# Block 0's heads transposed in pairs from one tile, masks of later blocks on GpSimd, no GpSimd power at the close

## The chip, the cores and the metric

The kernel runs on one core of a Trainium2 chip. A core has five engines with queues of their own, each worked off in order: TensorE (matrix products into PSUM), VectorE and ScalarE (elementwise work), GpSimd (elementwise work in SBUF, and DMA issue) and SyncE (DMA issue). The metric is the device time of one execution in microseconds; lower is better.

## The reference, cut to what matters

One decoder layer on 2048 tokens of width 1024, in float32. A joint projection feeds 8 stick-breaking attention heads (dimension 64) and 4 heads of gated linear attention; both outputs are normalised per head, joined, projected and added to the input; a ConvFFN follows and a last norm.

```python
def reference(x, ...):
    h = rms_norm(x, attn_norm_g[l])
    proj = h @ w_in[l]
    sb_q, sb_k, sb_v, g_q, g_k, g_v, g_lr, g_og = jnp.split(proj, offsets, axis=-1)
    o_sb = head_rms_norm(stick_breaking_attention(sb_q, sb_k, sb_v), sb_out_g[l])
    o_gla = head_rms_norm(gla_chunked(g_q, g_k, g_v, log_a), gla_out_g[l]) * jax.nn.silu(g_og)
    x = x + jnp.concatenate([o_sb, o_gla], axis=-1) @ w_out[l]
    h = rms_norm(x, ffn_norm_g[l])
    u = causal_depthwise_conv(h @ w_ffn_up[l], conv_w[l], conv_b[l])
    a, val = jnp.split(u, 2, axis=-1)
    x = x + (jax.nn.silu(a) * val) @ w_ffn_down[l]
    return rms_norm(x, final_norm_g)

def stick_breaking_attention(...):   # per block of queries; strict is s < t
    log1m = jnp.where(strict, -jax.nn.softplus(z), 0.0)
    after = lax.cumsum(log1m, axis=3, reverse=True) - log1m
    w = jnp.where(strict, jnp.exp(jax.nn.log_sigmoid(z) + after), 0.0)
    o = w @ v
```

## The kernel before, in words

Tokens are cut in 4 blocks of 512 (`NB`, `TB`), each in 4 row tiles of 128. Every float32 product is made of three passes over a high and a low half (`split_psum`, `split_w`: ScalarE rounds the high half, VectorE or GpSimd subtracts for the low one).

The stages follow each other: (1) norm of the input and transposes (`prep`, lines 189 to 208), where the norm's vector `gat` comes by GpSimd's DMA queue (line 195); (2) projections to DRAM, with the gated linear attention woven in (`gla`); (3) the output gate (`og_group`) of the 16 row tiles, with the attention of block 0 woven in from block 1 of the gate on; (4) for each block the output product, the FFN and the norm (`ffn`), with the attention of blocks 1 to 3 woven in by a running clock (lines 912 to 931).

Attention goes by steps (`attention_steps`). A step makes the weights of one row tile against one key block of 512: scores on TensorE, on the diagonal a matmul that adds a mask of -1e30 (line 529), two sigmoids on ScalarE (`m` and `wt`, lines 531 and 533), a product scan over `m` on VectorE (line 537) and `wt` times the scan (line 543). Five steps later (`LAG`) the weights are transposed (line 554), then multiplied with the values (lines 569 and 570). When a head is complete, `finish` transposes it back (line 580), squares it on GpSimd (585), takes mean and power there (86 and 88), scales it on VectorE (591), and SyncE stores it to the DRAM tile `osc` (593). Key and value tiles come by GpSimd's queue into a ring of buffers (line 517), as does the query (514).

`o_feat` makes the left operand of the output product: SyncE loads 128 of the 1024 features of a block from `osc` (line 620), TensorE transposes (623), and the halves are split (96 and 97). In block 0, `FEAT` says at which attention step and row tile each feature is made; feature 3 (heads 6 and 7) is made inside the output product (`LATE`, line 794).

`accumulate` is the output and the down product: two column halves `n`, eight (or seven) chunks `ci` of weights, each loaded, split and, in block 0, stored split for the later blocks (lines 720 to 731). Behind the last chunk VectorE adds the residual (765), ScalarE squares (768), VectorE sums (774), GpSimd raises to the power -0.5 (775), and `result` scales and stores.

TensorE's order is the program's. The queues of the other engines are ordered by a planner from simulated times, so an edit can re-order them elsewhere too.

Of the kernel before, what the change touches and what calls it, by code (L numbers as in the profile page):

```python
# [8 lines left out]
F32 = mybir.dt.float32  # L9
# [7 lines left out]
P = 128  # L17
# [25 lines left out]
FEAT = {4: (10, (2, 0)), 5: (12, (2, 0)), 6: (14, (2, 0)), 7: (16, (2, 0)),  # L43
        0: (26, (3, 0)), 1: (31, (3, 0)), 2: (38, (3, 0))}
# [5 lines left out]
def hybrid_block_kernel(ctx, tc, x, attn_norm_g, w_in, w_gate_up, b_gate_up, sb_out_g,  # L50
# [66 lines left out]
    if True:  # L117
# [11 lines left out]
        def n_tile(shape, name):  # L129
            return low.tile(shape, F32, tag="n", name=name, bufs=3)  # L130
# [55 lines left out]
        with tc.tile_pool(name="xp", bufs=2, side="right") as xp, tc.tile_pool(name="sm", bufs=2, side="right") as sm:  # L186
            gat = m1_tile([P, D], F32, "gat")

            def prep(b):
                for t in range(4):  # L190
# [3 lines left out]
                    if r0 == 0:  # L194
                        nc.gpsimd.dma_start(out=gat, in_=attn_norm_g.to_broadcast([P, D]))
# [108 lines left out]
        ams = [n_tile([P, 2, P], f"am{i}") for i in range(2)]  # L304
        for zt in [*qbd, *ams, *(sts[j][0] for j in range(NPAIR))]:
            nc.vector.memset(zt.bitcast(F32), 0.0)
# [165 lines left out]
    ohring = Ring([n_tile([P, 4, HD], f"oh{i}") for i in range(2)])  # L472
# [7 lines left out]
    def early_memory(q1):  # L480

        a0 = slot(0, [P, 4, TB], F32, "wtA")
        a1 = slot(1, [P, 4, TB], F32, "wtB")
        a2 = slot(2, [P, 2, 2, TB], F32R, "kvA")
        a3 = slot(3, [P, 2, 2, TB], F32R, "qA")
        tri = []
        for n, (whole, shared) in enumerate(((a0[:, 0, :], a0[:, 1, :]), (a0[:, 3, :], a1[:, 0, :]))):
            tri += [shared[:, 384:512], a0[:, 2, n * 256:(n + 1) * 256], shared[:, 0:384], whole]
        pring = Ring([a1[:, 2, :], a1[:, 3, :]])
        return ((Ring(tri), pring, Ring([a2[:, 0], a2[:, 1], a3[:, 1]]), Ring([q1, a3[:, 0]]), a1[:, 1, :]),  # L490
                (a0, a1, a2, a3, pring))
# [7 lines left out]
    def attention_steps(blocks, rings, behind=1, banks=None):  # L499
# [8 lines left out]
        def make_weights(u, t):  # L508
# [16 lines left out]
            for l in range(2):  # L525
                nc.tensor.matmul(z[:, :width], qt[:, l, t * P:(t + 1) * P], kt[:, 0, :width],  # L526
                                 start=(l == 0), stop=(l == 1 and not diag))
            if diag:
# [4 lines left out]
            nc.scalar.activation(wt[:, :width], z[:, :width], AF.Sigmoid, scale=0.125)  # L533
            pp = pring.next()[:, lo:TB]
# [41 lines left out]
        def finish(u, asb):  # L576
# [16 lines left out]
            nc.sync.dma_start(out=osc[i][:, h * HD:(h + 1) * HD].rearrange("(t p) d -> p t d", p=P), in_=oh)  # L593
# [20 lines left out]
    q1 = c1.enter_context(tc.tile_pool(name="q1", bufs=1, side="right")).tile([P, 2, TB], F32R, name="q1")  # L614
    early, shared = early_memory(q1)

    def o_feat(b, f, psum, tag, ot=None):
        if ot is None:
            ot = otring.next()
        nc.sync.dma_start(out=ot, in_=osc[b][:, f * P:(f + 1) * P].rearrange("(t p) d -> p t d", p=P))  # L620
# [16 lines left out]
    for b in range(NB):  # L637
        for t in range(4):
            for part, _ in enumerate(og_group(b, t)):
                if b > 0:  # L640

                    while steps < (16 * (b - 1) + 4 * t + part + 1) * FIRST // 46:
# [65 lines left out]
    def accumulate(lhs, w_rows, kept, b, squares=None, extra=None, stagger=False, rstds=None, rows=None, first=None):  # L708
# [5 lines left out]
        for n in range(2):  # L714
# [5 lines left out]
            def load(ci):  # L720
# [38 lines left out]
            for t in range(4):  # L759
# [6 lines left out]
                if squares is not None:  # L766
# [5 lines left out]
                    else:  # L772
                        r = rstds[0][:, t:t + 1]
                        nc.vector.tensor_tensor(out=r, in0=squares[:, t, 1:2], in1=squares[:, t, 0:1], op=ALU.add)
                        nc.gpsimd.tensor_tensor(out=r, in0=r, in1=nhalf[:, 0:1], op=ALU.pow)
                if R:
                    yield 0.65 * R

    def ffn(b, oT, rows, nextT):
# [51 lines left out]
        for gi, G in enumerate(GROUPS):  # L831
# [49 lines left out]
            yield from accumulate(gts, w_ffn_down[ch0 * P:(ch0 + G) * P, :], [w[ch0:ch0 + G] for w in wdn], b, squares=sq2 if final else None,  # L881
                                  extra=extra, stagger=final and last, rstds=[r2])
# [76 lines left out]
```

## Time and profile before

| | us |
|---|---|
| three timed runs | 2795.53, 2797.81, 2800.07 |
| median | 2797.81 |
| profiled execution | 2793.75 |
| its span, first to last instruction | 2791.8 |
| TensorE busy in the span | 2709.1 |

The profile shows one execution. The page gives the busy time of each engine and the costliest groups of instructions; the other views are lists of waits, windows of time, the chain of waits that ended last, and timelines. Matmuls are pipelined, so that a matmul's length is longer than its distance to the next one: the distance counts.

### The profile page before, as it was taken

The page shows a single profiled execution, that of the slowest core. Times are in us where ns is not written, and L with a number is a line of the kernel's source. Part 1 is how long each engine was busy: PE and PEld are TensorE (multiplying, and loading weights), DVE is VectorE, ACT ScalarE, POOL GpSimd, SP SyncE. Part 2 cuts the span into 40 slices and gives each one's busy share as a digit, 9 for nine tenths or more (in the row PEclk, how much of TensorE's full clock was granted, in tenths as well). Part 3 has the DMA queues.
Part 4 walks back from the last instruction along what each step waited for, and adds up shares of the span by engine and source line. Part 5 has one row for each costly group of instructions (what it writes and reads, how often), then busy time and mean ns, then how long its engine had stood idle before and what let it go on. Part 6 is the DMA issues. An engine that isn't in the chain of part 4 may idle for free.

```text
span 2791.8 us, 35920 instructions
## 1 busy us (share of the span) xinstructions
PE 2709.1 (97%) x13096; PEld 2249.1 (81%) x13096; DVE 1678.1 (60%) x2758; ACT 1144.5 (41%) x2364; POOL 542.7 (19%) x754
## 2 busy tenths in 40 slices
PE   8999999999799999999999999999999999999998
PEld 6878888878578778887888888888888888888886
DVE  5246755457487586777776777767767334342333
ACT  5455533235365355554443444445434222221112
POOL 2001212114455455433110000110100000000000
PEclk9999999999899999999999999999999999999999
DMA  6215635467567777768455455574454656555552
GB/s 187 94 62 175 232 136 160 115 184 247 210 210 249 248 238 245 244 232 286 153 185 187 165 181 168 184 250 157 170 175 161 221 191 222 206 196 194 193 192 75
DMA packets 260896, 529.00 MB, mean 189 GB/s; under 512 B 59152, under 2 KB 149360, under 8 KB 238192
## 3 DMA queue, kind: packets, MB, share of 16 engines
q1 hardware_dynamic: 229472, 389.86, 42.9%
q0 software_dynamic: 31248, 136.85, 13.7%
q8 instruction: 103, 1.69, 0.2%
q14 instruction: 73, 0.60, 0.1%
HBM read 384.04 MB, written 142.61 MB: 189 GB/s over the span
## 4 chain that ended last, share of the span: by engine, by line
PE 86%; DVE 5%; DMA 4%; POOL 2%; issue 1%; ACT 1%; SPq 0%; POOLq 0%; ACTq 0%; DVEq 0%
PE ups L848 11%; PE ups L849 11%; PE ups L850 11%; PE d L738 7%; PE d L739 7%; PE d L740 7%; PE z L526 4%; PE tp L554 4%; PE mm L166 3%; PE mm L164 3%; PE mm L165 3%; PE acc L570 2%; PE mm L176 2%; PE mm L175 2%; PE mm L174 2%; PE acc L569 2%
## 5 line engine op out<-in xcount | busy, mean ns | idle before, releaser
L848 PE MATMUL ups<-h2h,u 128*128 128x512 f32 x1408 | 554.3, 394 | 5.0 <-DVE x L765 5.0
L849 PE MATMUL ups<-h2l,u 128*128 128x512 f32 x1408 | 550.7, 391 | 0.0
L850 PE MATMUL ups<-h2h,u 128*128 128x512 f32 x1408 | 549.4, 390 | 0.0
L94 DVE TENSOR_TENSOR ws<-tp,ws 128x512 fp32r<-128x512 f32 (+1 forms) x320 | 194.1, 607 | 202.7 <-ACT ws L93 201.8
L848 PEld LDWEIGHTS ups<-h2h,u 128*128 128x128 f32 x1408 | 265.0, 188 | 61.6 <-DVE x L765 5.6
L850 PEld LDWEIGHTS ups<-h2h,u 128*128 128x128 f32 x1408 | 264.8, 188 | 57.5
L849 PEld LDWEIGHTS ups<-h2l,u 128*128 128x128 f32 x1408 | 265.0, 188 | 54.6
L738 PE MATMUL d<-d,g 128*128 128x512 f32 x736 | 292.0, 397 | 2.5 <-ACT d L101 1.2
L93 ACT ACTIVATE ws<-tp 128x512 fp32r<-128x512 f32 (+1 forms) x320 | 170.0, 531 | 293.9 <-PE tp L554 290.0
L739 PE MATMUL d<-d,g 128*128 128x512 f32 x736 | 288.9, 392 | 0.9 <-POOL d L102 0.9
L740 PE MATMUL d<-d,g 128*128 128x512 f32 x736 | 288.3, 392 | 0.0
L860 DVE SCALAR_TENSOR_TENSOR ct<-ups,cwb,ct 128x511 f32<-128x511 f32 x176 | 131.8, 749 | 251.1 <-POOL ct L859 197.3
L855 ACT ACTIVATE ct<-ups,cwb 128x512 f32<-128x512 f32 x176 | 136.3, 775 | 340.6 <-PE ups L850 340.4
L537 DVE TENSOR_TENSOR_SCAN wtB<-mt,cy 128x512 f32<-128x512 f32 x192 | 250.3, 1304 | 3.0 <-ACT mt L531 2.8
L765 DVE TENSOR_TENSOR x<-d,x 128x512 f32<-128x512 f32 x128 | 85.8, 685 | 165.5 <-PE d L740 165.4
L531 ACT ACTIVATE mt<-z 128x512 f32<-128x512 f32 (+2 forms) x320 | 170.5, 533 | 13.3 <-DVE cy L541 8.0
L859 POOL TENSOR_TENSOR ct<-ct,hadd 128x2 f32<-128x2 f32 x132 | 26.6, 202 | 744.5 <-ACT halo L857 332.4
L738 PEld LDWEIGHTS d<-d,g 128*128 128x128 f32 x736 | 138.4, 188 | 33.4 <-ACT d L101 1.6
L740 PEld LDWEIGHTS d<-d,g 128*128 128x128 f32 x736 | 138.4, 188 | 31.1
L739 PEld LDWEIGHTS d<-d,g 128*128 128x128 f32 x736 | 138.5, 188 | 30.5 <-POOL d L102 1.5
L164 PE MATMUL mm<-hh,w 128*128 128x512 f32 x384 | 151.3, 394 | 0.0
L165 PE MATMUL mm<-hl,w 128*128 128x512 f32 x384 | 150.2, 391 | 0.0
(242 smaller groups left out, 5341.9 us busy)
## 6 DMA issues: line engine op xcount, KB each, us to landing
u<-wup SPq DMA_DIRECT2D x132, 1024.0 KB, 4.7
d<-wdn SPq DMA_DIRECT2D x94, 512.0 KB, 3.4
wup<-u POOLq DMA_DIRECT2D x44, 1024.0 KB, 6.7
kvA<-kvs POOLq DMA_DIRECT2D x54, 512.0 KB, 4.8
uraw<-in_w_ffn_up_dram SPq DMA_DIRECT2D x44, 512.0 KB, 4.8
wdn<-d POOLq DMA_DIRECT2D x44, 512.0 KB, 4.9
d<-wou SPq DMA_DIRECT2D x38, 512.0 KB, 4.2
dw<-wdn SPq DMA_DIRECT2D x38, 512.0 KB, 3.8
```

Of the source, the lines that this page charges most:

```text
L93: nc.scalar.activation(hi, ps, AF.Copy)
L94: nc.vector.tensor_tensor(out=lo, in0=ps, in1=hi.bitcast(F32), op=ALU.subtract)
L164: nc.tensor.matmul(ps, whi[k][:, fs], hh[b][k // 4][:, k % 4, :], start=(k == 0), stop=False)
L165: nc.tensor.matmul(ps, whi[k][:, fs], hl[b][k // 4][:, k % 4, :], start=False, stop=False)
L531: nc.scalar.activation(m[:, lo:TB], z[:, :width], AF.Sigmoid, scale=-0.125)
L537: nc.vector.tensor_tensor_scan(out=pp[:, ::-1], data0=mr, data1=mr, initial=1.0 if prev is None else prev, op0=ALU.mult, op1=ALU.bypass)
L738: nc.tensor.matmul(accs[t], gh[:, ts], whi, start=(ci == 0), stop=False)
L739: nc.tensor.matmul(accs[t], gh[:, ts], wlo, start=False, stop=False)
L740: nc.tensor.matmul(accs[t], gw[:, ts], whi, start=False, stop=(ci == G - 1))
L848: nc.tensor.matmul(ps, whi[:, k, :], hk, start=(k == 0), stop=False)
L849: nc.tensor.matmul(ps, whi[:, k, :], lk, start=False, stop=False)
L850: nc.tensor.matmul(ps, wlo[:, k, :], hk, start=False, stop=(k == KT - 1))
```

## The change

- `finish` of block 0 leaves its output in one tile `ohp` of four row tiles by 128 features, the even head in the left 64 columns and the odd in the right; `o_feat` transposes features 0 to 3 of block 0 from that tile. The store to `osc` stays for blocks 1 to 3. `PAIRS` gives the steps for features 0 to 2; feature 3 stays in `LATE`. The gated features 4 to 7 are made one at a time (`GATED`).
- In blocks 1 to 3 the mask matmul goes; two selections on GpSimd set the masked part of `m` to 1 and of `wt` to 0 after the sigmoids.
- In the output product of block 0, half `n` = 0, the odd chunks' low halves are made by VectorE.
- In the last product of the last block the power on GpSimd becomes `root`: a square root on ScalarE, and a reciprocal with one correction on VectorE. The table for the root is loaded ahead by two one-column instructions. GpSimd's addition of the epsilon (line 770) stays.
- `gat` comes by ScalarE's DMA queue. Block 0's key/value ring gets a fourth buffer beside the query's. The two mask tiles of the gated attention become one tile.

```diff
-FEAT = {4: (10, (2, 0)), 5: (12, (2, 0)), 6: (14, (2, 0)), 7: (16, (2, 0)),
-        0: (26, (3, 0)), 1: (31, (3, 0)), 2: (38, (3, 0))}
+PAIRS = (8 + LAG + 5, 16 + LAG + 5, 24 + LAG + 5)
+GATED = {4: (2, 0), 5: (2, 1), 6: (3, 0), 7: (3, 1)}
...
-                        nc.gpsimd.dma_start(out=gat, in_=attn_norm_g.to_broadcast([P, D]))
+                        nc.scalar.dma_start(out=gat, in_=attn_norm_g.to_broadcast([P, D]))
...
-        ams = [n_tile([P, 2, P], f"am{i}") for i in range(2)]
+        am2 = n2_tile([P, 2, 2, P], "am")
+        ams = [am2[:, i] for i in range(2)]
...
-    ohring = Ring([n_tile([P, 4, HD], f"oh{i}") for i in range(2)])
+    ohp = n2_tile([P, 4, P], "ohp")
+    ohring = Ring([ohp[:, :, a * HD:(a + 1) * HD] for a in range(2)])
...
-        return ((Ring(tri), pring, Ring([a2[:, 0], a2[:, 1], a3[:, 1]]), Ring([q1, a3[:, 0]]), a1[:, 1, :]),
+        return ((Ring(tri), pring, Ring([kv1, a2[:, 0], a2[:, 1], a3[:, 1]]), Ring([q1, a3[:, 0]]), a1[:, 1, :]),
...
-                                 start=(l == 0), stop=(l == 1 and not diag))
-            if diag:
+                                 start=(l == 0), stop=(l == 1 and (i > 0 or not diag)))
+            if diag and i == 0:
                 nc.tensor.matmul(z[:, width - P:width], identr, mbias, start=False, stop=True)
...
+            if diag and i > 0:
+                for blk, fill in ((m[:, TB - P:TB], 1.0), (wt[:, width - P:width], 0.0)):
+                    nc.gpsimd.affine_select(out=blk, in_=blk, pattern=[[-1, P]], compare_op=ALU.is_gt,
+                                            fill=fill, base=0, channel_multiplier=1)
...
-            nc.sync.dma_start(out=osc[i][:, h * HD:(h + 1) * HD].rearrange("(t p) d -> p t d", p=P), in_=oh)
+            if i > 0:
+                nc.sync.dma_start(out=osc[i][:, h * HD:(h + 1) * HD].rearrange("(t p) d -> p t d", p=P), in_=oh)
...
-        if ot is None:
-            ot = otring.next()
-        nc.sync.dma_start(out=ot, in_=osc[b][:, f * P:(f + 1) * P].rearrange("(t p) d -> p t d", p=P))
+        if b == 0 and f < SBH // 2:
+            ot = ohp
+        else:
+            if ot is None:
+                ot = otring.next()
+            nc.sync.dma_start(out=ot, in_=osc[b][:, f * P:(f + 1) * P].rearrange("(t p) d -> p t d", p=P))
...
-                for f, (when, row) in FEAT.items():
-                    if f not in oT and steps >= when and (b, t) >= row:
-                        oT[f] = o_feat(0, f, pc, "c", ot=ots[len(oT) % 4])
+                    for f, when in enumerate(PAIRS):
+                        if f not in oT and steps >= when:
+                            oT[f] = o_feat(0, f, pc, "c")
+                for f, row in GATED.items():
+                    if f not in oT and (b, t) >= row:
+                        oT[f] = o_feat(0, f, pc, "c", ot=ots[f % 4])
...
-                    split_w(pair[:, 0, :], pair[:, 1, :], raw)
+                    split_w(pair[:, 0, :], pair[:, 1, :], raw, nc.vector if first and n == 0 and ci % 2 else nc.gpsimd)
...
-                        nc.gpsimd.tensor_tensor(out=r, in0=r, in1=nhalf[:, 0:1], op=ALU.pow)
+                        if final:
+                            root(r)
+                        else:
+                            nc.gpsimd.tensor_tensor(out=r, in0=r, in1=nhalf[:, 0:1], op=ALU.pow)
...
+    def root(r):
+        y = sm.tile([P, 2], F32, tag="rt", name="rt", bufs=4)
+        nc.scalar.activation(y[:, 0:1], r, AF.Sqrt)
+        nc.vector.reciprocal(out=y[:, 0:1], in_=y[:, 0:1])
+        nc.vector.tensor_tensor(out=y[:, 1:2], in0=y[:, 0:1], in1=y[:, 0:1], op=ALU.mult)
+        nc.vector.scalar_tensor_tensor(out=y[:, 1:2], in0=y[:, 1:2], scalar=-0.5, in1=r, op0=ALU.mult, op1=ALU.mult)
+        nc.vector.scalar_tensor_tensor(out=r, in0=y[:, 1:2], scalar=1.5, in1=y[:, 0:1], op0=ALU.add, op1=ALU.mult)
...
+            if final and last:
+                nc.scalar.activation(sq2[:, 3, 0:1], gts[-1][0][:, 0:1].bitcast(F32), AF.Square)
+                nc.scalar.activation(sq2[:, 3, 1:2], sq2[:, 3, 0:1], AF.Sqrt)
```

## Rows read from the trace of the kernel before

PE is TensorE, PEld its weight load, DVE VectorE, ACT ScalarE, POOL GpSimd, SP SyncE; a q behind the name is the engine's own queue. Times are us from the start of the span; in square brackets stands how long the engine was idle before the instruction and what ended that. In rows 3 the busy times stand in the order PE, PEld, DVE, ACT, POOL.

**Rows 1.** page, busy us of each engine (share of the span), instructions
```profile
PE 2709.1 (97%) x13096; PEld 2249.1 (81%) x13096; DVE 1678.1 (60%) x2758; ACT 1144.5 (41%) x2364; POOL 542.7 (19%) x754
```

**Rows 2.** waits of TensorE: us in total, times, longest
```profile
PE tpo L623 <- DMA kvB<-osc: 14.4, 2, 13.3
```

**Rows 3.** windows: length, busy us (instructions), clock, DMA share, GB/s
```profile
711.31:724.57 13.26, 0.00 (x1) 0.03 (x1) 0.00 (x0) 0.00 (x0) 3.21 (x5) 0.66 0.95 362
...
724.57:735.00 10.43, 10.43 (x40) 8.39 (x41) 6.04 (x8) 4.25 (x9) 0.37 (x1) 0.78 0.01 2
...
775.00:1270.00 495.00, 483.37 (x2385) 401.86 (x2386) 373.03 (x568) 270.43 (x539) 242.00 (x231) 0.99 0.71 240
...
1290.00:1850.00 560.00, 556.15 (x2744) 462.23 (x2743) 406.48 (x657) 248.92 (x526) 57.10 (x119) 1.00 0.55 182
```

**Rows 4.** chain of waits, 705 to 725 us: start, us, what
```profile
705.71 14.00 DMA osc<-oh
...
719.73 4.71 DMA kvB<-osc
```

**Rows 5.** timeline of the close: start, us, engine, instruction
```profile
2762.01 0.37 POOL L770 TENSOR_SCALAR sq<-sq 128x1 f32<-128x1 f32 x1 [0.88 <-ACT jk L768]
...
2781.30 0.55 POOL L775 TENSOR_TENSOR r<-r,nhalf 128x1 f32<-128x1 f32 x1 [1.64 <-DVE r L774]
...
2781.88 0.72 ACT L900 ACTIVATE yt<-x,r 128x512 f32<-128x512 f32 x1 [0.85 <-POOL r L775]
```

**Rows 6.** line 955: ns shortest/median/longest, first and last start
```profile
L955 POOLq DRAIN  x3: 46/102/9736, 2781.3 to 2791.5; - x3
...
L955 SPq DRAIN  x3: 7/7/7, 2785.4 to 2791.3; - x3
```

**Rows 7.** timeline of the first 14 us
```profile
6.33 0.57 POOL L88 TENSOR_TENSOR nr<-nm,nhalf 128x1 f32<-128x1 f32 x1
...
9.14 2.48 DVE L200 SCALAR_TENSOR_TENSOR xn<-xt,nr,gat 128x1024 f32<-128x1024 f32 x2 [6.79 <-DMA gat<-in_attn_norm_g_dram]
...
13.22 0.83 SPq L193 DMA_DIRECT2D xt<-in_x_dram  x2
```

**Rows 8.** timeline of TensorE, 704 to 711 us
```profile
704.20 0.50 PE L739 MATMUL d<-wsplit,g 128*128 128x512 f32 x1 [2.67 <-POOL wsplit L102]
...
710.92 0.39 PE L740 MATMUL d<-wsplit,g 128*128 128x512 f32 x1
```

**Rows 9.** timeline of GpSimd at 710 us
```profile
710.46 2.50 POOL L102 TENSOR_TENSOR wmore<-wraw,wmore 128x512 fp32r<-128x512 f32 x2
```

**Rows 10.** timeline of VectorE, 689 to 700 us
```profile
689.28 4.75 DVE L537 TENSOR_TENSOR_SCAN wtB<-mt 128x128 f32<-128x128 f32 x2
...
699.03 1.22 DVE L537 TENSOR_TENSOR_SCAN wtB<-mt 128x512 f32<-128x512 f32 x1
```

**Rows 11.** timeline of TensorE and VectorE, 670 to 680 us
```profile
670.52 0.30 PE L554 MATMUL tp<-ident,wtA 128*128 128x128 f32 x1
...
671.63 0.42 DVE L591 TENSOR_TENSOR oh<-oh,sbr 128x256 f32<-128x256 f32 x1 [1.00 <-POOL sbr L88]
...
679.64 0.63 PE L623 MATMUL tpo<-ident,wtC 128*128 128x128 f32 x4 [0.96 <-DMA wtC<-osc]
```

**Rows 12.** timeline of TensorE around one mask matmul
```profile
1529.85 0.22 PE L529 MATMUL z<-mbias,identr 128*128 128x128 f32 x1
1529.91 0.44 PE L738 MATMUL d<-d,g 128*128 128x512 f32 x1
1530.19 0.39 PE L739 MATMUL d<-d,g 128*128 128x512 f32 x1
1530.42 0.40 PE L740 MATMUL d<-d,g 128*128 128x512 f32 x1
```

**Rows 13.** groups by line on GpSimd: busy us, mean ns | idle before
```profile
L102 POOL TENSOR_TENSOR u<-uraw,u 128x1024 fp32r<-128x1024 f32 x44 | 107.6, 2446 | 103.5 <-ACT u L101 95.4 <-PE tp L554 7.8
...
masks.py:199 POOL TENSOR_SCALAR_AFFINE_SELECT ident<-ident 128x128 f32<-128x128 f32 x1 | 0.3, 312 | 0.1
```

More of the change, by code (lines that the diff above doesn't have):

```diff
@@ L129, in n_tile, with n2_tile @@
         def n_tile(shape, name):
-            return low.tile(shape, F32, tag="n", name=name, bufs=3)
+            return low.tile(shape, F32, tag="n", name=name)
+        def n2_tile(shape, name):
+            return low.tile(shape, F32, tag="n2", name=name)
         ev = c1.enter_context(tc.tile_pool(name="ev", bufs=2, side="right"))
@@ L303, in hybrid_block_kernel @@
         kTs = [[gst.tile([P, P], F32R, name=f"kT{i}{l}") for l in range(2)] for i in range(2)]
-        ams = [n_tile([P, 2, P], f"am{i}") for i in range(2)]
-        for zt in [*qbd, *ams, *(sts[j][0] for j in range(NPAIR))]:
+        am2 = n2_tile([P, 2, 2, P], "am")
+        ams = [am2[:, i] for i in range(2)]
+        for zt in [*qbd, am2, *(sts[j][0] for j in range(NPAIR))]:
             nc.vector.memset(zt.bitcast(F32), 0.0)
@@ L478, in hybrid_block_kernel, with early_memory @@
     nc.vector.tensor_copy(out=mbias, in_=mb0)
-    def early_memory(q1):
+    def early_memory(q1, kv1):
         a0 = slot(0, [P, 4, TB], F32, "wtA")
@@ L613, in hybrid_block_kernel @@
     ctx.enter_context(tc.manual_schedule(engines={mybir.EngineType.PE}))
-    q1 = c1.enter_context(tc.tile_pool(name="q1", bufs=1, side="right")).tile([P, 2, TB], F32R, name="q1")
-    early, shared = early_memory(q1)
+    qk1 = c1.enter_context(tc.tile_pool(name="q1", bufs=1, side="right")).tile([P, 2, 2, TB], F32R, name="qk1")
+    q1, kv1 = qk1[:, 0], qk1[:, 1]
+    early, shared = early_memory(q1, kv1)
     def o_feat(b, f, psum, tag, ot=None):
-        if ot is None:
-            ot = otring.next()
-        nc.sync.dma_start(out=ot, in_=osc[b][:, f * P:(f + 1) * P].rearrange("(t p) d -> p t d", p=P))
+        if b == 0 and f < SBH // 2:
[4 more added lines that the diff above has]
+            nc.sync.dma_start(out=ot, in_=osc[b][:, f * P:(f + 1) * P].rearrange("(t p) d -> p t d", p=P))
         tp = psum.tile([P, 4, P], F32, tag=tag, name="tpo")
@@ L640, in hybrid_block_kernel @@
                 if b > 0:
-                    while steps < (16 * (b - 1) + 4 * t + part + 1) * FIRST // 46:
+                    if steps < (16 * (b - 1) + 4 * t + part + 1) * FIRST // 46:
                         next(first, None)
                         steps += 1
-                for f, (when, row) in FEAT.items():
-                    if f not in oT and steps >= when and (b, t) >= row:
-                        oT[f] = o_feat(0, f, pc, "c", ot=ots[len(oT) % 4])
+                    for f, when in enumerate(PAIRS):
[4 more added lines that the diff above has]
+                        oT[f] = o_feat(0, f, pc, "c", ot=ots[f % 4])
             if (b, t) == (1, 3):
@@ L706, in after_attention, with accumulate @@
         return True
-    def accumulate(lhs, w_rows, kept, b, squares=None, extra=None, stagger=False, rstds=None, rows=None, first=None):
+    def accumulate(lhs, w_rows, kept, b, squares=None, extra=None, stagger=False, rstds=None, rows=None, first=None,
+                   final=False):
         G = len(lhs)
@@ L881, in ffn @@
             yield from accumulate(gts, w_ffn_down[ch0 * P:(ch0 + G) * P, :], [w[ch0:ch0 + G] for w in wdn], b, squares=sq2 if final else None,
-                                  extra=extra, stagger=final and last, rstds=[r2])
+                                  extra=extra, stagger=final and last, rstds=[r2], final=final and last)
             ch0 += G
```

## The prediction

> **What bounds the kernel now.** I read the page's busy times first: TensorE is busy 2709.1 of 2791.8 us [rows 1]. What the change can win lies in the 82.7 us in which it stands, in matmuls that go away, or in what follows the last matmul. The list of TensorE's waits puts one entry at the head: 14.4 us for a load of head outputs, 13.3 of them in one wait [rows 2]. The windows say where matmuls bound the time: from 1290 to 1850 us TensorE is busy 556.15 of 560 us, so there only fewer matmuls help; in block 0's FFN, 775 to 1270, it is busy 483.37 of 495 [rows 3].
>
> Three places belong to the edits. The chain of waits runs, from 705.71, over the store of head 7 to DRAM (14.00 us) and the load of its pair back (4.71 us); only then does TensorE transpose feature 3 [rows 4]. Behind the last matmul the end is set by GpSimd: a power, then a drain of 9.736 us [rows 5, 6]. At the start VectorE waits 6.79 us for the norm vector [rows 7].
>
> **Base of the sum.** Durations come from the profiled execution: 2793.75 us, of which 2791.8 are the span and 1.95 lie around it. The three timed runs have a median of 2797.81, 4.06 above it. I sum differences in the profile and take them off the median.
>
> **Part 1: pairs transposed from one tile.** The store and the load of features 0 to 3 go. For feature 3 TensorE stands from 711.31 (710.92 + 0.39 [rows 8]) to 724.57: 13.26 us, in which VectorE does nothing either [rows 3]. In the changed kernel it needs VectorE's product, which ends at 705.71, where the store now starts [rows 4]: the wait goes whole. With it goes its after-effect. The granted clock is 0.66 over the stand and 0.78 over the 10.43 busy microseconds behind it [rows 3]; 10.43 x 0.22 = 2.3 us. Together 15.6 us.
>
> What is late next? Chunk 6 of the output weights: its low half is the first of two GpSimd subtractions that start at 710.46 and take 2.50 us together [rows 9], so it is ready at 711.7. TensorE wants it after four transposes and a score, at about 712: just covered. The change also gives the odd chunks' subtractions to VectorE, each priced below a scan of the same width, 1.22 us [rows 10]; chunks 5 and 7 fall where VectorE stands, and GpSimd's even ones can only come sooner. Behind that come the second half's weights. The transfer queues were 95% busy at 362 GB/s in the stand and 1% busy after it [rows 3]: a backlog drained while TensorE waited. In the changed kernel the first chunks of that half are split long before, and the next loads are issued when chunk 0 has been multiplied, some 10 us after the backlog ends, so I count no loss. Bounds: 4 us won if such a load meets a backlog, takes the 14.00 us of the store with one chunk's 12 matmuls at 0.23 us as its only cover, and so costs 11.2 of the 15.6; 19 won if the 2.67 us wait for chunk 4's low half at 704.20 [rows 8] also goes with its slow clock, as GpSimd has less queued.
>
> The other pairs are transposed two steps after the step that begins their second head's norm. Head 5 is the tight one: TensorE then stands at about 670.6 (the last transpose starts at 670.52), and VectorE's product ends at 672.05 [rows 11], so it waits about 1.5 us. Against that, 0.96 us for feature 2's load at 679.64 go [rows 11]. Net 0.5 lost, between 3 lost and 1 won. Spreading the gated features 4 to 7 over four rows of tiles keeps their loads and transposes; the fourth key/value buffer brings the first score forward, but a stall behind it has a cause that isn't touched. For these and the merged memset I take nothing.
>
> **Part 2: masks.** 128 matmuls add the mask (4 tiles, 8 heads, 4 blocks); block 0 keeps 32, so 96 go. One takes 0.06 us before the next matmul starts, and that one's successor comes after 0.28 us, where 0.23 is usual [rows 12]: 0.11 us each, 10.6 us in all where TensorE is the bound. The price is 192 selections on GpSimd. The nearest row is the one that builds the identity, of the same shape: 0.312 us [rows 13], 60 us in all, and GpSimd is busy only 542.7 us [rows 1]. What could cost is latency: ScalarE, GpSimd, then VectorE's scan. The cover is the five steps between the weights and their transposes. In blocks 2 and 3 GpSimd works 57.10 of 560 us [rows 3]. In block 0's FFN, where block 1's 32 diagonal steps run, it works 242.00 of 495 [rows 3], in order: a selection can sit behind a weight subtraction of 2.446 us [rows 13]. VectorE's scan then waits, and behind it the convolutions that free TensorE's PSUM. VectorE has 122 us to spare there (495 - 373.03 [rows 3]). I take 8.5 won; the best bound is 10.6, the worst a loss (rival C).
>
> VectorE is also slower while GpSimd works. Two narrow scans that start at 689.28 take 4.75 us beside GpSimd's subtractions; one of full width takes 1.22 us at 699.03 [rows 10]. The Trainium skill, SBUF — State Buffer, section "SBUF: two separate sides", says that the two engines lock a shared port pair against each other for a whole instruction when VectorE reads two SBUF inputs. That rule speaks against this edit, and the trace agrees with it; at 0.31 us a selection it would hold VectorE for 60 us at most, spread over three blocks, and the sum by it stays the same as long as that is idle time.
>
> **Part 3: the close.** GpSimd's last power starts at 2781.30 [rows 5]. Its drain starts in the same moment and lasts 9.736 us, to 2791.0, though SyncE's first drain, behind the last output's landing, stands at 2785.4 [rows 6]. After 2791.0 there are 0.8 us to the end. If the drain belongs to GpSimd's last work, then with that work at 2762.01 [rows 5] it is over before 2773, and the end is 2785.4 + 0.8 = 2786.2: 5.6 us won. The new root is one ScalarE and four VectorE instructions of one column in a row; against the 0.58 us from the power's start to the product that uses it [rows 5] I take 0.4 us more, and only on the last tile. Its table is loaded ahead, behind ScalarE's last rounding, while TensorE runs the last down product and ScalarE has nothing to do. Net 5.2; bounds 0.4 lost and 5.6 won.
>
> **Part 4: norm vector.** The first scale is ready at 6.90 (6.33 + 0.57), VectorE starts at 9.14 [rows 7]; 2.2 us is the most. But the next row tiles' loads are issued by SyncE at 13.22 [rows 7], behind six small loads, and don't move, so TensorE's second stop stays where it is. ScalarE issues the new load before its first square, while that waits for the input. I take 0.3; bounds 0 and 2.2.
>
> **Sum.** 15.6 - 0.5 + 8.5 + 5.2 + 0.3 = 29.1 us; 2797.8 - 29.1 = 2768.7, rounded 2769.
>
> **Rivals.**
> A. The drain is not tied to GpSimd's last work: part 3 gives -0.4, the time is 2774. For it: nothing in the profile shows what the drain waits for. Against: it outlasts the last landing by 5.6 us in which no other work is shown.
> B. The wait for feature 3 turns into one for weights, or for head 7's norm, which is queued on GpSimd among the weights. Part 1 gives 4 in place of 15.1: 2780. For it: the full transfer queues. Against: 1% in the window after.
> C. Slower. Each of the 32 diagonal steps in block 0's FFN finds both its selections behind a subtraction: 2 x 2.446 = 4.9 us a step in which VectorE's in-order queue stands. Its idle time pays 122/32 = 3.8 us a step. The other parts' 20.6 us and the masks of blocks 2 and 3 (64 x 0.11 = 7.0) pay another 0.9, so from 4.7 us a step on the kernel is slower. At 4.9: 32 x 1.1 = 35 lost, 27.6 won, 2805. For it: GpSimd also stands at key/value loads until buffers are free. Against: GpSimd is idle half the time there, so few steps meet two.
> D. The edits work, and one of the re-ordered queues gains a stall of their size: 2798. For it: every queue but TensorE's is laid out anew. Against: only the one stall of that size exists now.
>
> **How the numbers follow.** Forecast 0.52, A 0.18, B 0.17, C 0.07, D 0.06. A and B together give 2785. With every part at its better bound the gain is 19 + 1 + 10.6 + 5.6 + 2.2 = 38.4, 2759. The range, 2756 to 2788, holds the forecast, A and B; C and D lie outside. A measurement of this kernel tells 0.2%, 5.6 us, from no change. Faster is the forecast, A and B: 0.87. Slower is C and a little of D: 0.08; same is the rest of D: 0.05.
>
> **What would show it.** Right: no transfer ahead of feature 3's transposes and a granted clock near 1 from 700 to 735 us; 32 mask matmuls left; GpSimd's long drain over before the last output lands; idle TensorE in block 0's FFN still near 12 us. Wrong: TensorE waits of several us for weights in the output product; VectorE waiting on selections for over 1 us each, and TensorE on VectorE behind them; a drain that ends 10 us after the close began, as now.

## The result, and the profile after

The changed kernel takes 2766.11 us (median of 4 runs, 2761.78 to 2773.36), the kernel before, beside it, 2798.94 (2795.53 to 2801.18): a ratio of 0.9894, 95% interval 0.9877 to 0.9911. The profiled execution has 2762.93 us, of which 2761.2 are the span, 30.6 less than before. Run again beside the experiments ("the control"), it took 2765.01, ratio 0.9893 (0.9878 to 0.9908).

I read the two traces by stages, each from one first matmul to another. "og" is first score to first output-product matmul, "product + FFN 0" from there to block 1's first upcast transpose, "FFN 1 + 2" from there to block 3's, "last FFN" from there to the start of the last matmul, "close" from there to the end of the span. Edges are rounded, so a value can be 0.1 us off.

| profile | og | product + FFN 0 | FFN 1 + 2 | last FFN | close | span |
|---|---|---|---|---|---|---|
| before | 116.0 | 666.6 | 1052.8 | 368.9 | 13.3 | 2791.8 |
| after | 111.9 | 653.1 | 1048.6 | 369.0 | 8.8 | 2761.2 |
| control | 112.5 | 656.5 | 1048.1 | 369.0 | 8.8 | 2766.7 |
| pairs by DRAM | 115.2 | 670.0 | 1048.1 | 370.7 | 9.0 | 2784.6 |
| masks by matmul | 113.7 | 649.7 | 1052.4 | 370.7 | 8.4 | 2764.1 |
| one late GpSimd copy | 115.0 | 655.7 | 1048.2 | 369.0 | 14.3 | 2773.7 |
| vector by GpSimd's queue | 111.9 | 646.3 | 1048.3 | 370.6 | 8.9 | 2759.1 |
| three key/value buffers | 113.0 | 647.2 | 1048.8 | 369.0 | 8.9 | 2760.6 |
| chunk 6's low half, VectorE | 114.8 | 647.2 | 1048.6 | 370.6 | 8.5 | 2761.4 |
| two heads' masks by matmul | 112.0 | 649.3 | 1048.5 | 370.6 | 8.5 | 2758.3 |
| chunk 6 whole, VectorE | 113.9 | 652.1 | 1048.5 | 369.0 | 8.5 | 2762.2 |
| weight loaded twice | 115.4 | 657.5 | 1048.4 | 369.0 | 8.7 | 2770.3 |
| twice, and chunk 6 whole | 113.6 | 660.8 | 1048.8 | 369.0 | 8.5 | 2771.5 |
| chunk 6 whole, two heads | 113.8 | 645.2 | 1048.0 | 370.6 | 8.9 | 2757.7 |

FFN 1 + 2 agree to within 0.8 us wherever the kernels agree there, the last FFN to within 1.7; og scatters by 3.5 us, and product + FFN 0 by far more. That stage is where the question lies.

The page after, busy times, against [rows 1]: TensorE 12.8 us less, GpSimd 68 more.

```profile
PE 2696.3 (98%) x13000; PEld 2235.0 (81%) x13000; DVE 1686.7 (61%) x2777; ACT 1146.3 (42%) x2371; POOL 610.7 (22%) x937
```

Waits of TensorE after (us in total, times, longest), four of the first ten. Against [rows 2], the wait of 14.4 for head outputs is down to 2.3, in later blocks; the wait for chunk 6 of the output weights (`wmore`) is new, in two parts.

```profile
PE ups L881 <- DVE x L786: 3.9, 1, 3.9
PE d L760 <- POOL wmore L103: 3.6, 1, 3.6
...
PE tpo L640 <- DMA kvB<-osc: 2.3, 2, 1.3
...
PE d L759 <- ACT wmore L102: 1.8, 1, 1.8
```

How these two waits come about is read from the timelines of ScalarE, GpSimd and TensorE after, 692 to 707 us (start, us, instruction, idle before and its releaser).

```profile
694.87 0.63 ACT L102 ACTIVATE wmore<-wraw 128x512 fp32r<-128x512 f32 x1
700.50 1.06 ACT L102 ACTIVATE u<-uraw 128x1024 fp32r<-128x1024 f32 x1 [5.00 <-DMA uraw<-in_w_ffn_up_dram]
701.46 0.61 ACT L102 ACTIVATE wmore<-wraw 128x512 fp32r<-128x512 f32 x1
...
692.53 1.26 POOL L103 TENSOR_TENSOR wsplit<-wraw,wsplit 128x512 fp32r<-128x512 f32 x1
...
701.64 2.36 POOL L103 TENSOR_TENSOR u<-uraw,u 128x1024 fp32r<-128x1024 f32 x1 [3.69 <-ACT u L102]
703.95 2.18 POOL L103 TENSOR_TENSOR wmore<-wraw,wmore 128x512 fp32r<-128x512 f32 x1
...
693.84 0.50 PE L760 MATMUL d<-wsplit,g 128*128 128x512 f32 x1 [0.88 <-POOL wsplit L103]
...
702.12 0.50 PE L759 MATMUL d<-wmore,g 128*128 128x512 f32 x1 [1.84 <-ACT wmore L102]
...
706.18 0.80 PE L760 MATMUL d<-wmore,g 128*128 128x512 f32 x1 [3.56 <-POOL wmore L103]
```

ScalarE's queue is in order. It stands 5.00 us at the rounding of an up-projection weight of block 0, the third, whose load has not landed, and chunk 6's rounding stands behind that. GpSimd then subtracts the weight first, 2.36 us, and chunk 6 second. (693.84 is the wait for chunk 4's low half, 2.67 us in [rows 8].) Feature 3 itself, where TensorE stood before, is in time: head 7's product starts at 694.07 on VectorE, and its pair's transposes end before 700 with no wait.

The windows that answer to [rows 3], and the output product (its first matmul to block 0's first upcast transpose) after:

```profile
755.00:1250.00 495.00, 481.14 (x2346) 398.03 (x2347) 374.46 (x567) 270.85 (x539) 270.71 (x310) 0.99 0.71 241
1270.00:1830.00 560.00, 557.16 (x2737) 462.46 (x2736) 410.32 (x662) 249.83 (x529) 86.16 (x186) 1.00 0.55 184
...
681.70:751.60 69.90, 60.08 (x263) 47.70 (x262) 43.11 (x61) 28.32 (x62) 42.62 (x57) 0.93 0.68 248
```

In FFN 0 TensorE is idle 13.9 of 495 us (495 - 481.14), against 11.6 in [rows 3]; in FFN 1 it stays the bound. The close, against [rows 5, 6]: the last row tile's output and the drains, of line 992 now.

```profile
2756.64 0.72 ACT L937 ACTIVATE yt<-x,r 128x512 f32<-128x512 f32 x1 [1.00 <-DVE r L810]
...
L992 POOLq DRAIN  x3: 40/102/9482, 2735.8 to 2760.9; - x3
L992 SPq DRAIN  x3: 7/7/7, 2760.4 to 2760.7; - x3
```

GpSimd's long drain begins at 2735.8 and is over at 2745.3; SyncE's first drain at 2760.4 now sets the end.

### The profile page after: what moved, and what is told of

The parts are those of the page before. It is cut to its first block, busy times and chain, and to the rows that moved or that the text cites. A ratio compares the mean times of both kernels' runs of the same rounds, so it can differ in the third digit from the quotient of the medians.

```text
span 2761.2 us, 36066 instructions
## 1 busy us (share of the span) xinstructions
PE 2696.3 (98%) x13000; PEld 2235.0 (81%) x13000; DVE 1686.7 (61%) x2777; ACT 1146.3 (42%) x2371; POOL 610.7 (22%) x937
## 4 chain that ended last, share of the span: by engine, by line
PE 85%; DVE 5%; DMA 4%; POOL 2%; ACT 2%; issue 2%; SPq 1%; ACTq 0%; POOLq 0%; DVEq 0%
PE ups L881 11%; PE ups L882 11%; PE ups L883 11%; PE d L760 6%; PE d L759 6%; PE d L761 6%; PE z L533 4%; PE tp L566 4%; PE mm L170 2%; PE mm L169 2%; PE mm L168 2%; PE acc L582 2%; PE mm L179 2%; PE mm L180 2%; PE mm L178 2%; PE acc L581 2%
## 5 line engine op out<-in xcount | busy, mean ns | idle before, releaser
L168 PE MATMUL mm<-hh,w 128*128 128x512 f32 x384 | 151.2, 394 | 0.0
L170 PE MATMUL mm<-hh,w 128*128 128x512 f32 x384 | 149.4, 392 | 0.8 <-POOL w L103 0.8
```

Source lines behind the costliest of these rows:

```text
L168: nc.tensor.matmul(ps, whi[k][:, fs], hh[b][k // 4][:, k % 4, :], start=(k == 0), stop=False)
L170: nc.tensor.matmul(ps, wlo[k][:, fs], hh[b][k // 4][:, k % 4, :], start=False, stop=(k == KT - 1))
```

## The experiments

Times are medians. The twelve runs stand in three sets of four, in the order below, each with the kernel before on the same chip (2794.53, 2792.96 and 2796.51); ratios are to that, and from set to set the ratios compare, not the times. The stages come from one profile of each run.

**Control: the changed kernel again.** No edit.

> The changed kernel again, unaltered, as the base that the other kernels of this group are set against on the same chip. Every theory: 2761 to 2773 us, as in its first four runs, and stages of the profile within 2 us of its first profile (start of block 0's FFN transposes at 751.6 us, block 1's at 1334.8, block 2's at 1899.9, block 3's at 2383.4).

2765.01, ratio 0.9893 (0.9878 to 0.9908). The time is as expected, the stages are not: block 0's FFN transposes start at 757.4 us, 5.8 later than in the first profile. The waits for chunk 6 are 4.82 and 3.27 us, with 7.93 of ScalarE's wait ahead of them.

**Part 1 undone.** The pairs go through DRAM again, and all features are made at the steps of `FEAT` again.

```diff
-PAIRS = (8 + LAG + 5, 16 + LAG + 5, 24 + LAG + 5)
-GATED = {4: (2, 0), 5: (2, 1), 6: (3, 0), 7: (3, 1)}
+FEAT = {4: (10, (2, 0)), 5: (12, (2, 0)), 6: (14, (2, 0)), 7: (16, (2, 0)),
+        0: (26, (3, 0)), 1: (31, (3, 0)), 2: (38, (3, 0))}
...
-            if i > 0:
+            if True:
                 nc.sync.dma_start(out=osc[i][:, h * HD:(h + 1) * HD]...
...
-        if b == 0 and f < SBH // 2:
-            ot = ohp
-        else:
+        if True:
...
```

> The changed kernel with part 1 undone alone: block 0's heads are stored to DRAM and loaded back again, at the old steps. Theory of the prediction (the 13.26 us wait for feature 3 with its slow clock is what part 1 removed, less what is late next): 11 to 15 us slower than the changed kernel, with a TensorE wait of 10 us or more for a load ahead of feature 3's transposes. Rival B (the wait only changed its name): 4 us slower or less. Rival E (the early 7 us that TensorE gained before 600 us come from fewer transfers on SyncE's queue): the start of block 0's attention slips back by 5 us too, so 17 to 20 us slower in all.

2782.74, ratio 0.9953 (0.9936 to 0.9970): 17.7 us above the control, 13.5 of them in product + FFN 0. The wait is back, TensorE's timeline of this kernel:

```profile
720.38 1.09 PE L638 MATMUL tpo<-ident,kvB 128*128 128x128 f32 x4 [15.94 <-DMA kvB<-osc]
```

The rest of the 17.7 is 2.7 in og and 1.7 in the last FFN, which scatter by as much; block 0's attention starts at 571.6 us, against 571.8 in the control, so rival E's slip did not come. Part 1 is the larger half of the change.

**Part 2 undone.** All masks by matmul.

```diff
-                                 start=(l == 0), stop=(l == 1 and (i > 0 or not diag)))
-            if diag and i == 0:
+                                 start=(l == 0), stop=(l == 1 and not diag))
+            if diag:
...
-            if diag and i > 0:
+            if False:
```

> The changed kernel with part 2 undone alone: all 128 mask matmuls, no selection after the sigmoids. Theory of the prediction: 0.11 us for each of 96 matmuls less 2 us of hidden cost, so 8.5 us slower than the changed kernel. Rival (read from the two profiles: the stages from block 0's FFN on became 0.7, 3.5 and 0.8 us shorter for 46, 30 and 12 masks): about 5 us slower, because in block 0's FFN TensorE gets the time back as waits; then blocks 1 and 2 lengthen by 0.11 us a mask and block 0's FFN stage by under 1 us.

2768.08, ratio 0.9906 (0.9893 to 0.9918): 3.1 above the control by the medians, and the intervals overlap. FFN 1 + 2 are 4.3 us longer than in the control; product + FFN 0 is 6.8 shorter, and the wait for chunk 6 is gone: ScalarE waits only 2.55 us for the weight there. So by the times this run does not show that part 2 pays; what shows it is FFN 1 + 2, a stage that repeats within 0.8 us. The wait made me suspect the selections.

**Part 3 undone in its effect.** One GpSimd copy of a column behind the last root.

```diff
                         if final:
                             root(r)
+                            if t == 3:
+                                z_ = sm.tile([P, 1], F32, tag="zl", name="zl", bufs=1)
+                                nc.gpsimd.tensor_copy(out=z_, in_=r)
```

> The changed kernel with one more GpSimd instruction at the very end: it copies the last row tile's root, one column, into a tile that nobody reads. No engine waits for it. Theory (the drain of 9.5 us follows GpSimd's last instruction): the drain starts at the copy, some 9.5 us before the end, and the span becomes 5 to 6 us longer, 2766.5 for 2761.2. Rival A (the drain is not tied to the last instruction, it ended early for another reason): no difference.

2773.74, ratio 0.9928 (0.9913 to 0.9943), 8.7 above the control by the medians. The close takes 14.3 us in place of 8.8, and that is what the edit can change. The copy and the drains of this kernel:

```profile
2763.66 0.19 POOL L800 COPY zl<-r 128x1 f32<-128x1 f32 x1 [20.44 <-DVE r L813]
...
L995 POOLq DRAIN  x3: 40/93/9286, 2763.6 to 2773.4; - x3
```

A copy of 0.19 us moves the end by 5.5. The drain belongs to GpSimd's last work, and rival A is out.

**Selections of two heads taken away.** The 16 selections that GpSimd executes ahead of the output product's end become matmuls again.

```diff
+    def by_matmul(i, h):
+        return i == 0 or (i == 1 and h < 2)
...
-            if diag and i == 0:
+            if diag and by_matmul(i, h):
...
-            if diag and i > 0:
+            if diag and not by_matmul(i, h):
```

> The masks of block 1's first two heads, whose 16 selections GpSimd executes in the output product of block 0, are added by matmul again (like block 0's); all other masks stay with GpSimd. Theory (the selections delay what stands behind them in GpSimd's and ScalarE's queues, and so chunk 6's halves): from the first output-product matmul to the first upcast transpose about 64 us, as with all masks by matmul (63.7), in place of 69.9 to 73.1; the later stages stay as in the changed kernel (583, 565, 483); 8 matmuls more cost about 1 us; the time is 6 to 8 us below the changed kernel, about 2758. Rival (the waits for chunk 6 come from the transfer of the first up-projection weights, and the 63.7 was chance): 70 to 73 us in that stretch, the time 2765 to 2767.

2760.81, ratio 0.9881 (0.9869 to 0.9894). The time is near the theory's, but not for its reason: the output product takes 68.5 us, not 64, and two kernels below that keep all selections do better in product + FFN 0 (647.2 and 646.3, against 649.3). TensorE no longer waits for chunk 6, but it waits 2.92 us for chunk 4 ahead of it, in place of 0.8; chunk 6's low half is ready 20.5 us after the product's first matmul, and 20.4 in the kernel with the vector on GpSimd's queue, which keeps the selections. So the selections' own time on GpSimd does not make chunk 6 late.

Their removal does change when the weight lands. SyncE issues the third up-projection weight 6.8 us after the product's first matmul, in place of 3.8, and it takes 7.5 us to land, in place of 15.0. SyncE's row (it merges the third and the fourth load) and the landing of the third, after and then in this kernel:

```profile
685.46 5.08 SPq L875 DMA_DIRECT2D uraw<-in_w_ffn_up_dram  x2
...
DMA to landing us min/median/max: 15.0/15.0/15.0
```

```profile
688.21 2.45 SPq L878 DMA_DIRECT2D uraw<-in_w_ffn_up_dram  x2
...
DMA to landing us min/median/max: 7.5/7.5/7.5
```

So the transfer is late, as the rival says, and the order of the queues that the selections bring is a likely part of it.

**Chunk 6's low half by VectorE.**

```diff
-                    split_w(pair[:, 0, :], pair[:, 1, :], raw, nc.vector if first and n == 0 and ci % 2 else nc.gpsimd)
+                    split_w(pair[:, 0, :], pair[:, 1, :], raw, nc.vector if first and n == 0 and (ci % 2 or ci == 6) else nc.gpsimd)
```

> Chunk 6's low half of the output weights is subtracted by VectorE instead of GpSimd; all else as in the changed kernel. Theory (TensorE's second wait for chunk 6, 3.3 to 3.6 us, is GpSimd finishing the subtraction of an up-projection weight first): that wait goes, the first one (1.8 to 4.8 us, for ScalarE's rounding behind another that waits for a transfer) stays; the output product takes 66 to 69 us in place of 69.9 to 73.1, the time is 2 to 4 us below the changed kernel, about 2762. Rival (the chunk is late as a whole, and VectorE has scans ahead of it): the wait becomes one for VectorE of about the same size; within 1 us of the changed kernel.

2760.11, ratio 0.9876 (0.9861 to 0.9890). The wait for GpSimd goes; 1.9 us for VectorE stand in its place. The wait for ScalarE's rounding, which was to stay, is gone too, and the output product takes 63.2 us, under the 66 to 69 forecast, at a granted clock of 1.00 where the profile after has 0.93. ScalarE waits only 2.80 us for the weight in this profile, so part of it may be luck.

**Three key/value buffers again.**

```diff
-Ring([kv1, a2[:, 0], a2[:, 1], a3[:, 1]])
+Ring([a2[:, 0], a2[:, 1], a3[:, 1]])
...
```

> The key/value ring of block 0's attention has three buffers again, as in the kernel before; all else as changed. Theory (the fourth buffer is worth nothing; the 4 us that went between the first score and the output product came with the pairs): that stretch stays at 112 us, within 1.5, and the time within 3 us of the changed kernel. Rival (the fourth buffer gave the 4 us): the stretch goes back to about 116 us, the time to about 2769.

og takes 113.0 us: the fourth buffer did not give the 4 us. The time, 2770.98 (2760.32 to 2776.32), ratio 0.9912 (0.9894 to 0.9931), scatters by 16 us and decides nothing.

**Norm vector by GpSimd's queue again.**

```diff
-                        nc.scalar.dma_start(out=gat, ...
+                        nc.gpsimd.dma_start(out=gat, ...
```

> The norm vector is loaded by GpSimd's queue again, as in the kernel before. Theory of the prediction (0.3 us from this edit, as the next row tiles' loads are not moved): TensorE starts 1.0 us later (10.5 in place of 9.5 us), but the end of the first projections moves by 0 to 1 us; the time is within 1 us of the changed kernel. Rival (the whole second of the start arrives at the end): 1 to 2.2 us more, about 2766 to 2767; the profile's first matmul and last matmul move by the same.

2762.61 (2760.38 to 2775.8), ratio 0.9900 (0.9882 to 0.9919). Its first transpose starts at 9.90 us, against 9.49. The timelines of the first 10 us, after and then of this kernel:

```profile
6.04 1.06 ACT L202 ACTIVATE xn<-xt 128x1024 f32<-128x1024 f32 x1 [3.52 <-DMA xt<-in_x_dram]
...
8.15 1.28 DVE L204 SCALAR_TENSOR_TENSOR xn<-xt,nr,gat 128x1024 f32<-128x1024 f32 x1 [5.80 <-POOL nr L89]
```

```profile
4.47 1.06 ACT L202 ACTIVATE xn<-xt 128x1024 f32<-128x1024 f32 x1 [2.38 <-DMA xt<-in_x_dram]
...
8.56 2.48 DVE L204 SCALAR_TENSOR_TENSOR xn<-xt,nr,gat 128x1024 f32<-128x1024 f32 x2 [6.21 <-DMA gat<-in_attn_norm_g_dram]
```

By ScalarE's queue the vector is in time, but the first input tile's square starts 1.57 us later, and VectorE waits for its scale instead: of the 2.2 us at most, 0.4 is left. The square starts at 5.93 to 6.15 us in all twelve profiles with the vector on ScalarE's queue, and at 4.47 and 4.83 in the two with GpSimd's.

This kernel and the one with three buffers differ from the control only in stages that lie earlier, and yet take 646.3 and 647.2 us in product + FFN 0. What differs along with that is when the weight lands. The five profiles with the changed kernel's code in that stage, by ScalarE's wait for the weight: 0.2 us, 646.3; 1.9, 647.2; 5.0, 653.1; 6.1, 655.7; 7.9, 656.5. The shortest of these, ScalarE's timeline with the vector on GpSimd's queue:

```profile
698.19 0.63 ACT L102 ACTIVATE wmore<-wraw 128x512 fp32r<-128x512 f32 x1
699.04 1.06 ACT L102 ACTIVATE u<-uraw 128x1024 fp32r<-128x1024 f32 x1 [0.22 <-DMA uraw<-in_w_ffn_up_dram]
700.01 0.61 ACT L102 ACTIVATE wmore<-wraw 128x512 fp32r<-128x512 f32 x1
```

The last four runs take that link apart.

**Chunk 6 whole by VectorE.** Neither half stands behind the weight.

```diff
-    def split_w(hi, lo, raw, eng=nc.gpsimd):
-        nc.scalar.activation(hi, raw, AF.Copy)
+    def split_w(hi, lo, raw, eng=nc.gpsimd, by=None):
+        if by is None:
+            nc.scalar.activation(hi, raw, AF.Copy)
+        else:
+            by.tensor_copy(out=hi, in_=raw)
...
-                    split_w(pair[:, 0, :], pair[:, 1, :], raw, nc.vector if first and n == 0 and ci % 2 else nc.gpsimd)
+                    split_w(pair[:, 0, :], pair[:, 1, :], raw, nc.vector if first and n == 0 and (ci % 2 or ci == 6) else nc.gpsimd,
+                            by=nc.vector if first and n == 0 and ci == 6 else None)
```

> VectorE makes both halves of chunk 6 of the output weights (the rounding as a copy, then the subtraction), so that neither stands behind the third up-projection weight on ScalarE or GpSimd. All else as in the changed kernel. In the runs so far, the stretch from the output product's first matmul to block 1's first upcast transpose takes 646.3, 647.2, 653.1, 655.7 and 656.5 us where ScalarE waits 0.2, 1.9, 5.0, 6.1 and 7.9 us for that weight's transfer. Theory (chunk 6 is late because it stands behind that weight): 645 to 648 us however long ScalarE waits; all five times between 2756 and 2764, median about 2760. Rival (a late transfer slows the stretch in other ways too, by the sigmoids behind it on ScalarE): the stretch still follows the wait, above 650 where it is 5 us or more, and some times lie above 2768.

2758.62 (2755.35 to 2763.95), ratio 0.9864 (0.9848 to 0.9880), the lowest median of all. In its profile ScalarE waits 7.41 us, and TensorE does not wait for chunk 6 at all; the output product takes 66.3 us, against 73.1 in the control at 7.93. But product + FFN 0 takes 652.1, not 645 to 648: 4.4 less than the control, and not independent of the wait. The times are the theory's, the stage is the rival's.

**The weight loaded twice**, so that it lands later.

```diff
-                        nc.sync.dma_start(out=raw, in_=wuv[:, s, :, c * P:(c + 1) * P])
+                        for _ in range(2 if (c, s) == (1, 0) else 1):
+                            nc.sync.dma_start(out=raw, in_=wuv[:, s, :, c * P:(c + 1) * P])
```

> The third up-projection weight of block 0 is loaded twice in a row to the same place (the second load waits for the first), so that it lands later; the result is the same. All else as in the changed kernel, chunk 6's high half behind it on ScalarE. Theory: a transfer that is later by one landing, 4 to 12 us, makes ScalarE's wait that much longer, and the stretch from the output product to block 1's first upcast transpose 4 to 12 us longer than in the changed kernel (653 to 657): 657 to 669, the time 2769 to 2777. Rival (wait and stretch only go together, through something else): the wait grows and the stretch stays at 646 to 657.

2769.76, ratio 0.9897 (0.9881 to 0.9914), stage 657.5: within the theory's numbers. But the order on ScalarE came out otherwise, and chunk 6's rounding is ahead of the weight's. TensorE still loses 7.73 us. The timelines of ScalarE, VectorE and TensorE of this kernel:

```profile
699.91 1.15 ACT L102 ACTIVATE wmore<-wraw 128x512 fp32r<-128x512 f32 x2
716.55 1.06 ACT L102 ACTIVATE u<-uraw 128x1024 fp32r<-128x1024 f32 x1 [10.02 <-DMA uraw<-in_w_ffn_up_dram]
...
718.12 0.69 DVE L95 TENSOR_TENSOR ws<-tp,ws 128x512 fp32r<-128x512 f32 x1 [9.79 <-ACT ws L94]
718.73 0.68 DVE L786 TENSOR_TENSOR x<-d,x 128x512 f32<-128x512 f32 x1
...
719.46 0.80 PE L759 MATMUL d<-d,g 128*128 128x512 f32 x1 [7.73 <-DVE x L786]
```

ScalarE's 10.02 us become VectorE's 9.79: its subtraction of a transposed weight needs the rounding that is queued on ScalarE behind the up-projection weight. Behind that subtraction VectorE has the addition that frees the first accumulator, and TensorE's next product needs this accumulator.

**Both edits at once**, the diffs of the last two.

> Both edits at once: the third up-projection weight loaded twice, and chunk 6 made by VectorE alone. Theory: ScalarE waits as long as with the double load, but chunk 6 does not stand behind it: the stretch takes 645 to 650 us, the time is at most 3 us above the kernel with chunk 6 on VectorE alone. Rival (the sigmoids behind the same wait are what TensorE misses): 655 us or more, within 3 us of the double load alone.

2771.93, ratio 0.9907 (0.9892 to 0.9922), stage 660.8, the same wait of 7.4 us for the addition. The theory, that only chunk 6 suffers, falls. The numbers are the rival's, but not its reason: what VectorE waits for, 9.50 us, is again the rounding of a transposed weight, not a sigmoid.

**Chunk 6 whole by VectorE, and two heads' masks by matmul**, the two diffs above.

> The two remedies together: chunk 6 made by VectorE alone, and the masks of block 1's first two heads added by matmul. Theory (once chunk 6 no longer stands behind the transfer, the selections of those two heads cost nothing): within 2 us of the kernel with chunk 6 on VectorE alone, about 2760, or 1 us above it for 8 matmuls more. Rival (the selections in GpSimd's queue cost on their own, between VectorE's scans): 3 us or more below it, about 2756.

2762.02, ratio 0.9873 (0.9858 to 0.9887): 3.4 above chunk 6 alone by the medians, less by the ratio, with overlapping intervals. The theory's time does not come out within its 2 us by the medians, but the selections cost nothing here that these runs can tell. The weight lands at 14.4 us after the product's first matmul, and product + FFN 0, 645.2, is the shortest of all.

## Why the prediction was right, and where not

The total, 2769, is 3 us from the median, and the gain, 29.1 forecast, is 32.8 by the medians of the first runs and 29.5 by the control's. The mechanisms of the parts 1 and 3 are the ones named, and undoing each brought its cost back. But the close fit is partly luck. By the two profiles, product + FFN 0 won 6.6 us less than the sum has for it, and the stages ahead of it won 8.5 us where the sum has 0.2 lost; most of that second error is scatter.

**Part 1.** The wait for feature 3 went whole, as the sum has it, and undoing it costs 17.7 us against 15.1 forecast. What failed is the step "What is late next? [...] just covered". With the masks it won, product + FFN 0 should have gained 15.6 + 51 x 8.5 / 96 = 20.1 us (51 of the 96 mask matmuls start there in the trace before); it gained 13.5 after and 10.1 in the control, and 20.3 only where the weight lands early. Chunk 6's low half was ready 21.5 us after the product's first matmul before (711.7 less 690.2) and 24.4 after (706.1 less 681.7), because the weight ahead of it landed 18.8 us behind that matmul in place of 15.7, though it was issued earlier, and GpSimd took 2.18 us for the chunk where it took 1.29 before. TensorE came for the chunk at 18.6 (702.12 less 1.84 of wait, less 681.7), where 21.8 was forecast (712 less 690.2): the wait for chunk 4 ahead of it is 0.88 us in place of 2.67, and the granted clock behind that wait is 1.00 (693.84 to 699.21 us) where it was 0.76 (704.20 to 711.30 us). What stood among the better bounds thus came in part, and brought TensorE to chunk 6 too early. I priced GpSimd's subtraction and left out what is queued ahead of it, on ScalarE above all. The bounds of 4 to 19 held it. Of the signs, a granted clock near 1 from 700 to 735 us did not come (it is 0.90), and a sign of being wrong did, waits of several us for weights in the output product.

**Pairs.** Head 5 should have cost 1.5 us; no wait for a head's product is left in og. The stage is 4.1 us shorter, where I expected 0.5 longer. But twelve other profiles lie between 111.9 and 115.4, with the pairs through DRAM at 115.2, so most of this is scatter and no edit can be named for it. The same holds for the stretch up to the first score at 574 us, 4.4 us shorter after, where 0.3 was forecast.

**Part 2.** The price of a mask was right: in FFN 1, 30 mask matmuls start in the profile before, and TensorE's busy time falls by 3.57 us, 0.12 each; in FFN 2 it is 11 and 1.17, 0.11 each. FFN 1 + 2 gain 4.2 in time. In FFN 0, with 47 of them and not the 32 that the prediction puts there, 5.2 were to be won by that price: TensorE is idle 18.9 to 20.2 us there in the five profiles of the changed code, against 18.1 before and 16.7 with all masks by matmul, so about 1 to 3.5 of it are given back in waits. Undone, the part is worth 3.1 us in time, under the 8.5 taken, within its bounds and not clear of the scatter. Rival C did not come: VectorE's scans wait 11.9 us in all for selections, in 19 waits, the longest 2.3. The rows of their line after (the last one is idle time ahead of them):

```profile
L549 DVE TENSOR_TENSOR_SCAN wtB<-mt,cy x192: 1265/1275/2022, 703.3 to 2134.2; 128x512 f32<-128x512 f32 x192
...
  POOL mt L544: 11.9, 19
```

The selections' own price, against [rows 13] (busy us, mean ns | idle before): a mean of 317 ns on the first operand as forecast, but of 417 to 567 on the second, 80 us in all and not 60.

```profile
L544 POOL TENSOR_SCALAR_AFFINE_SELECT mt<-mt 128x128 f32<-128x128 f32 x96 | 30.5, 317 | 146.3 <-ACT mt L538 142.2 <-DVE ws L95 3.9
...
L544 POOL TENSOR_SCALAR_AFFINE_SELECT wtC<-wtC 128x128 f32<-128x128 f32 x45 | 22.2, 493 | 2.3 <-ACT wtC L540 1.7
L544 POOL TENSOR_SCALAR_AFFINE_SELECT wtA<-wtA 128x128 f32<-128x128 f32 x38 | 21.5, 567 | 1.7 <-ACT wtA L540 1.0
```

**Part 3.** 4.5 us by the close, where 5.2 stood. The drain behaves as forecast. The new root is the difference: the last output's start follows the last matmul's by 0.9 us more, not 0.4.

**Part 4.** 0.3 taken, 0.4 measured at the first transpose against the vector on GpSimd's queue, and 1.0 against the profile before; that the first input tile would land later was not foreseen. Later stages scatter too much to show what of it arrives.

**Rivals.** A is out by the late copy. B's kind of wait was there at half its price: 5.4 us for chunk 6 after and 8.1 in the control, where B lost 11. D came in a small way: the queues were laid out anew, and a load that the wait for feature 3 had covered now showed.

What stays open: why one and the same program's times lie up to 16 us apart. The stage moves by 10 us with the weight's landing from profile to profile and would explain it, but there is one profile to a kernel, and the run that made the weight land later also changed ScalarE's order, so this is argued and not shown. The queues' order seems to have a hand in it. In the eight profiles that keep all selections and load the weight once, it is issued 3.8 us after the product's first matmul and lands anywhere from 14.0 to 21.7 us after it, and the times of each run, four to six, spread over 6.1 to 16.0 us. In the three with the masks of block 1's first two heads by matmul it is issued at 6.8 and lands at 14.3 or 14.4, and the four or five times spread over 2.5, 3.6 and 4.8 us. Why the load that is issued earlier takes longer was not tested.

The lowest median keeps the change and makes chunk 6 on VectorE: 2758.62, 0.9864 of the kernel before. It lies 6.4 us below the control by the medians and 8 by the ratios, with intervals that just touch; the kernels with chunk 6's low half on VectorE (0.9876), with two heads' masks by matmul (0.9881) and with both remedies (0.9873) cannot be told from it.

## What to carry to other kernels

When a long wait goes, list what stands in each in-order queue ahead of the next operand, and which of those entries waits for a transfer: here one load that was not urgent held the operand behind it, and through ScalarE and VectorE the accumulators too. The price of a mask matmul in a row of the trace held in the stages where TensorE is the bound; in the stage with waits, 1 to 3.5 of 5.2 us came back as other waits. And look at which GpSimd instruction is the last: here the end of the program hung on it, and one late copy moved it by 5.5 us.

## What the runs showed of the hardware

GpSimd's drain at the end starts with its last instruction and takes 9.3 to 9.7 us in all fourteen profiles: 9.736 behind a power, 9.482 behind a column's addition, 9.286 behind a copy of 0.19 us; the end moved from 8.8 to 14.3 us behind the last matmul for that copy.

GpSimd's subtraction of 128x512 took 1.26 us at 692.53 and 2.18 at 703.95, where VectorE ran a scan of full width that took 1.72 us against 1.22 in [rows 10]. The scan after:

```profile
703.35 1.72 DVE L549 TENSOR_TENSOR_SCAN wtB<-mt,cy 128x512 f32<-128x512 f32 x1
```

The Trainium skill, SBUF — State Buffer, section "SBUF: two separate sides", gives a shared port pair that either engine holds for its whole instruction while the other stands, where VectorE has two SBUF inputs; the rows agree, for either engine.
